# Moving the middle half groups of the down projection among the products of an FFN pass on one Trainium2 core

## The chip, the core and the metric

The kernel runs on one core of a Trainium2 chip. The metric is the device time of one execution in microseconds (us); lower is better. TensorE multiplies matrices into PSUM, VectorE and ScalarE read PSUM and do the elementwise work, GpSimd has a small part, and SyncE (SP) issues the DMAs that bring weights from HBM.

## The reference

A two-layer trunk over 528 tokens (16 meta tokens and 512 inputs) of width 1024. Layer 0 has a sparse attention, layer 1 a differential attention, and each layer ends with the same gated FFN with a causal convolution of width 3. The change concerns that FFN alone:

```python
def conv_ffn(h, w_up, conv_w, conv_b, w_down):      # w_up: 1024 x 5632, w_down: 2816 x 1024
    u = h @ w_up
    up = jnp.pad(u, ((0, 0), (CONV_W - 1, 0), (0, 0)))
    c = conv_b + sum(up[:, j:j + Tp] * conv_w[j] for j in range(CONV_W))
    gate, val = jnp.split(c, 2, axis=-1)
    return (jax.nn.silu(gate) * val) @ w_down
```

## The kernel before

Activations lie with features on the 128 partitions and tokens along the free dimension. Float32 products are made of three matmuls each, from a high and a low part of either operand: a cast on ScalarE gives the high part (`hi`, L168), a subtraction on VectorE the low one (`lo`, L176).

The FFN has 22 blocks of 128 features f. Blocks 0 and 1 are computed plainly; f = 2 to 21 go through `up_pair(f)`, one pass for each. A pass computes the gate block and the value block of f together, for two halves of the tokens, by seven products in place of eight (the scheme of Strassen and Winograd). A product (`product`, its matmuls are L1240) is 4 steps in the contraction of three matmuls: 12 matmuls of 264 columns in layer 0, of 258 in layer 1. The names used here, in the order before the change:

- P1: G times the first half of the inputs, into g0. ScalarE then copies g0 to v0 (L1270), so that later products can add to it.
- P5: the sum weights S12 times input sums, into g1. ScalarE copies g1 to the tile p5 (L1274).
- P6: the other half of S12, added onto v0. VectorE then sets g1 = v0 + p5 (L1279).
- P2: the other half of G, added onto g0.
- P3: S34, onto v0; VectorE then sets v1 = v0 + p5 (L1296).
- P4: S34, onto g1. Now g is finished and goes through the convolution (`convolve`: ScalarE L1328, VectorE L1331).
- P7, the last product: half of the value weights (A22), onto v0. Then v is convolved.

g0 and g1 are two halves of one PSUM tile g, in two of its banks; v0 and v1 likewise of v.

While the passes run, the down projection of finished blocks is done beside them. `down(p, m)` multiplies four finished blocks by one of the 8 output blocks m, in two half groups of two blocks, and then adds the result to h on VectorE (L1385). It is a generator: the first `next` issues the first half group, the second `next` the other half, the third the addition. A half group (its matmuls are L1374) is 12 matmuls in layer 0, where the 528 tokens are taken in two pieces of 272 and 256 columns, and 6 of 512 columns in layer 1. Passes f = 5 to 20 have a "middle" pair of half groups (`at_mid`, generator `a`), passes f = 4 to 19 a "late" pair (`at_late`, generator `b`), one half behind P4 and one behind P7.

Inside the passes the order on TensorE, VectorE and ScalarE is the order of the code (`manual_schedule`, L1453); the other engines are ordered by the scheduler of the framework. The weights are handled by two objects of class `Weights`: `wt` for G, S12 and S34, `ws` for the half groups and A22, each with three buffers in turn for the raw weights, the high parts and the low parts. `early` issues the cast on ScalarE, `late` the low part on VectorE, `sum` two of the additions that make S12 and S34 (L137 and L138, L141 and L142), `take` hands weights to a product, `done` gives their buffers back, and a load is issued on SP (L115) when its raw buffer is free.

Of the kernel before, what the change touches and what calls it, by code (L numbers as in the profile page):

```python
# [229 lines left out]
def mm_cost(n):  # L230
    return n / 2400 + 0.003


class Trunk:
# [929 lines left out]
    def ffn(self, l):  # L1164
# [4 lines left out]
        wt, ws, x = self.wt, self.wsm, self.next_x  # L1169
# [5 lines left out]
        with self.pool("fp") as fp:  # L1175
# [61 lines left out]
            def product(out, w, wk, xs, xk, c0, first=True):  # L1237
                for k in range(4):
                    for p, (wi, xi) in enumerate(((0, 0), (0, 1), (1, 0))):
                        nc.tensor.matmul(out, w[wi][:, wk + k, :], xs[xi][:, xk + k, c0:c0 + N],  # L1240
                                         start=(first and k == 0 and p == 0), stop=(k == 3 and p == 2), skip_group_check=not first)
                    self.pe(3 * mm_cost(N))
                    self.poll()

            def up_pair(f):

                x0, x1 = x[0][2:], x[1][2:]
                off = 512 - mid
                more = f + 1 < NF
                n3, ns = wt.taken, ws.taken
                a, b = ((z.get(f) and down(*z[f])) or iter(()) for z in (at_mid, at_late))
                g = ps.tile([128, 1024], F32, tag="sp", name="g")
                g0, g1 = g[:, off + st0:512], g[:, 512:512 + N]
                for i in range(ns, ns + (f in at_mid) + (f in at_late) + 1):  # L1260
                    ws.early(i)
                before = rest.pop(f - 1, iter(()))
                next(before, None)
                while ws.half:
                    ws.late()
                G, S12 = wt.take(), wt.take()
                product(g0, G, 0, x0, 0, st0)
                v = ps.tile([128, 1024], F32, tag="sp", name="v")
                v0, v1 = v[:, off + st0:512], v[:, 512:512 + N]
                nc.scalar.copy(v0, g0)  # L1270
                next(before, None)
                product(g1, S12, 0, TT[0], 0, 0)
                p5 = fp.tile([128, 264], F32, tag="p", name="p5", bufs=2)[:, :N]
                nc.scalar.copy(p5, g1)  # L1274
                if more:
                    wt.sum()
                next(a, None)
                product(v0, S12, 4, TT[1], 0, 0, False)
                nc.vector.tensor_tensor(g1, v0, p5, op=OP.add)  # L1279
                if more:  # L1280
                    wt.sum()
                product(g0, G, 4, x0, 4, st0, False)
                wt.done()
                wt.done()
                wt.early(n3 + 3)
                wt.late()
                wt.early(n3 + 4)
                next(a, None)
                next(a, None)
                if f in at_mid:  # L1290
                    ws.done()
                if f + 1 in at_mid:
                    ws.early(ws.taken + (f in at_late) + 1)
                S34 = wt.take()
                product(v0, S34, 0, TT[2], 0, 0, False)
                nc.vector.tensor_tensor(v1, v0, p5, op=OP.add)  # L1296
                wt.late()
                ws.late()
                product(g1, S34, 4, x1, 4, mid - 264, False)
                wt.done()  # L1300
                convolve(g, f, 0, off)
                wt.early(n3 + 5)
                wt.late()
                next(b, None)
                nc.scalar.activation(conv[0][:, :n], conv[0][:, :n], AF.Silu)
                A22 = ws.take()
                product(v0, A22, 0, TT[3], 0, 0, False)
                convolve(v, f, 1, off)
                next(b, None)
                if f in at_late:  # L1310
                    ws.done()
                ws.done()
                rest[f] = finish_pair(f, conv[0], conv[1], b)
# [3 lines left out]
            def finish_pair(f, c, t, b):  # L1317
                nc.vector.tensor_tensor(c[:, :n], c[:, :n], t[:, :n], op=OP.mult)
                next(b, None)
                yield  # L1320
                split_acts(f, c)
                yield

            def convolve(u, f, e, off=240):
                j = f + NF * e
                w0, w1, w2, b = (par[:, cb + 44 * q + j:cb + 44 * q + j + 1] for q in range(4))
                t = conv[e] = fp.tile([128, T], F32, tag=f"c{e}", name=f"c{e}", bufs=2)
                nc.scalar.activation(t[:, :n], u[:, off + t0:off + T], AF.Identity, bias=b, scale=w2)  # L1328
                for d, w in ((1, w1), (2, w0)):
                    z = d if l == 0 else 0  # L1330
                    nc.vector.scalar_tensor_tensor(t[:, z:n], u[:, off + t0 + z - d:off + T - d], w, t[:, z:n],  # L1331
                                                   op0=OP.mult, op1=OP.add)
# [66 lines left out]
            def down(p, m):  # L1399
                f0, f1 = self.PARTS[p]  # L1400
                t, w = new(), ws.take()
                for k in range(f1 - f0):
                    if k == (f1 - f0) // 2:
                        yield
                    block(t, w, f0 + k, k, cols, k == 0, k == f1 - f0 - 1)
                yield
                add(t, m, cols, False)
                yield
# [34 lines left out]
            at_late, at_mid = self.down_slots()  # L1443
# [9 lines left out]
            with self.tc.manual_schedule(engines=ENGINES):  # L1453
                for f in range(self.PLAIN, NF):
                    up_pair(f)
                for _ in rest.pop(NF - 1):
                    pass
# [479 lines left out]
```

## Time and profile before

| | |
|---|---|
| median of 3 runs | 1424.27 us (1422.84 to 1425.43) |
| the profiled execution | 1424.05 us |
| its span | 1422.2 us |
| TensorE matmul busy | 1303.1 us (92%) |
| VectorE busy | 1076.8 us (76%) |
| ScalarE busy | 689.8 us (49%) |
| granted TensorE clock, mean | 0.977 |

The span is the time from the first to the last instruction that the profiler saw; the execution's own time has some 1.9 us around it. Passes f = 5 to 20 lie at 350 to 632 us in layer 0 and at 1097 to 1371 us in layer 1. In a timeline row, the text in brackets at the end is the time that the engine stood idle ahead of the instruction, with the instruction that it waited for. Matmuls are pipelined: each row is longer than the distance to the next start, and its end is modelled.

### The profile page before, as it was taken

How to read it: one execution, taken by the hardware profiler on the slowest of the kernel's cores; microseconds unless marked ns; L12 is line 12 of the kernel's file. 1: busy time of each engine (PE TensorE's matmuls, PEld its weight loads, DVE VectorE, ACT ScalarE, POOL GpSimd, SP SyncE). 2: the span in 40 equal slices, each digit the busy share in tenths (PEclk: the TensorE clock that was granted, in tenths of full speed). 3: DMA queues.
4: the chain of work that ended last, by engine and by line, in shares of the span. 5: the costliest groups of instructions: out<-in, count | busy, mean ns of one | idle time of the engine just before them, and what ended most of it. 6: DMA issues, size and time to landing. Idle time of an engine off the chain costs nothing.

```text
span 1422.2 us, 24955 instructions
## 1 busy us (share of the span) xinstructions
PE 1303.1 (92%) x9688; PEld 1238.2 (87%) x9688; DVE 1076.8 (76%) x2126; ACT 689.8 (49%) x1330; POOL 286.8 (20%) x334
## 2 busy tenths in 40 slices
PE   5999899988999999989799999999888999999988
PEld 4999788887999999989799999989787888888886
DVE  6499977788888888876657777665888888888873
ACT  4453555564444444444445555554564444444441
POOL 3404442400000000003444552445400000000000
PEclk9999999999999999999999999989999999999999
DMA  7312221221223322213222322112222332223212
GB/s 227 116 60 85 74 84 57 82 82 60 91 90 89 94 91 91 75 55 103 90 66 80 91 66 69 48 34 86 79 82 61 102 90 92 89 90 95 83 56 93
DMA packets 49302, 118.98 MB, mean 84 GB/s; under 512 B 6192, under 2 KB 15712, under 8 KB 49184
## 3 DMA queue, kind: packets, MB, share of 16 engines
q1 hardware_dynamic: 48432, 114.57, 26.2%
q0 software_dynamic: 752, 2.82, 0.6%
q8 instruction: 76, 1.25, 0.4%
q14 instruction: 42, 0.34, 0.1%
HBM read 112.46 MB, written 4.91 MB: 83 GB/s over the span
## 4 chain that ended last, share of the span: by engine, by line
PE 77%; DVE 13%; ACT 5%; issue 3%; POOL 1%; DMA 1%; SPq 0%; ACTq 0%; DVEq 0%; POOLq 0%
PE lin L306 20%; PE g L1240 17%; PE dn L1374 17%; PE v L1240 12%; DVE c L1331 2%; PE pv L1742 1%; PE stq L681 1%; DVE g L1279 1%; DVE lo L176 1%; PE pv L1119 1%; ACT v L1270 1%; PE linh L306 1%; DVE acc L560 1%; ACT hi L168 1%; DVE xl L630 1%
## 5 line engine op out<-in xcount | busy, mean ns | idle before, releaser
L306 PE MATMUL lin<-xh,hi 128*128 128x256 f32 (+3 forms) x928 | 271.9, 298 | 13.0 <-DVE ht L547 6.4
L306 PE MATMUL lin<-xl,hi 128*128 128x256 f32 (+3 forms) x928 | 272.0, 294 | 3.3 <-DVE xl L630 1.7
L306 PE MATMUL lin<-xh,lo 128*128 128x256 f32 (+3 forms) x928 | 271.6, 294 | 0.0
L168 ACT CAST hi<-raw 128x1024 fp32r<-128x1024 f32 (+3 forms) x225 | 181.5, 822 | 176.6 <-PE v L1240 81.9
L176 DVE TENSOR_TENSOR lo<-raw,hi 128x512 fp32r<-128x512 f32 (+3 forms) x196 | 177.8, 922 | 21.0 <-ACT hi L168 18.1
L306 PEld LDWEIGHTS lin<-xh,hi 128*128 128x128 f32 (+1 forms) x928 | 179.1, 195 | 16.7 <-ACT xh L656 8.5
L306 PEld LDWEIGHTS lin<-xl,hi 128*128 128x128 f32 (+1 forms) x928 | 180.9, 195 | 5.0 <-DVE xl L630 3.1
L306 PEld LDWEIGHTS lin<-xh,lo 128*128 128x128 f32 (+1 forms) x928 | 180.9, 195 | 0.0
L1240 PE MATMUL g<-xh,hi 128*128 128x264 f32 (+1 forms) x480 | 140.7, 293 | 30.8 <-DVE g L1279 24.1
L1374 PE MATMUL dn<-al,hi 128*128 128x256 f32 (+2 forms) x528 | 142.7, 321 | 0.0
L1374 PE MATMUL dn<-ah,lo 128*128 128x256 f32 (+2 forms) x528 | 142.4, 321 | 0.0
L1374 PE MATMUL dn<-ah,hi 128*128 128x256 f32 (+2 forms) x528 | 142.3, 321 | 0.0
L1240 PE MATMUL v<-Th,lo 128*128 128x264 f32 (+1 forms) x480 | 136.3, 284 | 0.0
L1240 PE MATMUL v<-Tl,hi 128*128 128x264 f32 (+1 forms) x480 | 136.2, 284 | 0.0
L1240 PE MATMUL v<-Th,hi 128*128 128x264 f32 (+1 forms) x480 | 135.9, 283 | 0.0
L1240 PE MATMUL g<-xl,hi 128*128 128x264 f32 (+1 forms) x480 | 135.8, 283 | 0.0
L1240 PE MATMUL g<-xh,lo 128*128 128x264 f32 (+1 forms) x480 | 135.8, 283 | 0.0
L1240 PEld LDWEIGHTS g<-xh,hi 128*128 128x128 f32 x480 | 90.3, 188 | 40.9 <-DVE g L1279 32.5
L168 ACT CAST hi<-S 128x1024 fp32r<-128x1024 f32 x80 | 83.5, 1043 | 49.5 <-PE g L1240 48.1
L1385 DVE TENSOR_TENSOR ht<-dn,ht 128x256 f32<-128x256 f32 (+2 forms) x120 | 58.2, 514 | 54.2 <-PE dn L1374 54.2
L176 DVE TENSOR_TENSOR lo<-S,hi 128x1024 fp32r<-128x1024 f32 x80 | 97.3, 1217 | 0.0
L1374 PEld LDWEIGHTS dn<-ah,lo 128*128 128x128 f32 x528 | 89.1, 188 | 7.6
(299 smaller groups left out, 3257.5 us busy)
## 6 DMA issues: line engine op xcount, KB each, us to landing
raw<-w_up SPq DMA_DIRECT2D x88, 512.0 KB, 3.6
raw<-w_down SPq DMA_DIRECT2D x64, 256.0 KB, 2.7
raw<-w_in SPq DMA_DIRECT2D x16, 512.0 KB, 3.6
raw<-w_kv SPq DMA_DIRECT2D x16, 512.0 KB, 3.6
raw<-w_down SPq DMA_DIRECT2D x16, 384.0 KB, 3.2
nb<-nbias SPq DMA_DIRECT2D x16, 264.0 KB, 2.8
raw<-w_o_a SPq DMA_DIRECT2D x8, 512.0 KB, 3.7
raw<-w_q SPq DMA_DIRECT2D x8, 512.0 KB, 3.5
```

Of the source, the lines that this page charges most:

```text
L168: nc.scalar.copy(hi[:, :n, :m], src)
L176: eng.tensor_tensor(lt[:, :n, :m], src, hi[:, :n, :m].bitcast(F32), op=OP.subtract)
L306: i = self.nc.tensor.matmul(o, w[wi][:, kw + k, :m], x[s][xi][:, kx + k, c0:HN[s]], start=(first and p == 0), stop=(last and p == 2))
L560: eng.tensor_tensor(acc, acc, sq[:, :n], op=OP.add)
L630: i = eng.tensor_tensor(xl[:, m, o:o + n], xfs[m][:, :n], xh[:, m, o:o + n].bitcast(F32), op=OP.subtract)
L681: self.nc.tensor.matmul(st[:, c:c + 2], sq[:, c0:c0 + 128], rhs, start=True, stop=True)
L1119: nc.tensor.matmul(pv[:, :4 * nq], v[:, c, :], pp[:, :, :nq], start=(ci == 0 and p == 0), stop=(ci == nch - 1 and p == 2))
L1240: nc.tensor.matmul(out, w[wi][:, wk + k, :], xs[xi][:, xk + k, c0:c0 + N], start=(first and k == 0 and p == 0), stop=(k == 3 and p == 2), ...
L1270: nc.scalar.copy(v0, g0)
L1331: nc.vector.scalar_tensor_tensor(t[:, z:n], u[:, off + t0 + z - d:off + T - d], w, t[:, z:n], op0=OP.mult, op1=OP.add)
L1374: nc.tensor.matmul(part(t, c0, c1, o), w[wi][:, k, :], acts[f][ai][:, c0:c1], start=(first and p == 0), stop=(last and p == 2))
L1385: nc.vector.tensor_tensor(hv, part(t, c0, c1, o), hv, op=OP.add)
```

## The change

In each pass the first middle half group moves from behind P5 to the place in front of P5, and the second half group, with the addition to h that follows it, moves from behind P2 to the place in front of P2. The order of groups becomes P1, half group, P5, P6, half group, P2. The calls on `ws` that stood behind the second half group (`done`, the `early` for the next pass's middle weights) move with it, and the `ws.late()` that belongs to this `early` moves there from its place behind the addition of v1.

```diff
                 nc.scalar.copy(v0, g0)
                 next(before, None)
+                next(a, None)
                 product(g1, S12, 0, TT[0], 0, 0)
                 p5 = fp.tile([128, 264], F32, tag="p", name="p5", bufs=2)[:, :N]
                 nc.scalar.copy(p5, g1)
                 if more:
                     wt.sum()
-                next(a, None)
                 product(v0, S12, 4, TT[1], 0, 0, False)
                 nc.vector.tensor_tensor(g1, v0, p5, op=OP.add)
                 if more:
                     wt.sum()
+                next(a, None)
+                next(a, None)
+                if f in at_mid:
+                    ws.done()
+                if f + 1 in at_mid:
+                    ws.early(ws.taken + (f in at_late) + 1)
+                    ws.late()
                 product(g0, G, 4, x0, 4, st0, False)
                 wt.done()
                 wt.done()
                 wt.early(n3 + 3)
                 wt.late()
                 wt.early(n3 + 4)
-                next(a, None)
-                next(a, None)
-                if f in at_mid:
-                    ws.done()
-                if f + 1 in at_mid:
-                    ws.early(ws.taken + (f in at_late) + 1)
                 S34 = wt.take()
                 product(v0, S34, 0, TT[2], 0, 0, False)
                 nc.vector.tensor_tensor(v1, v0, p5, op=OP.add)
                 wt.late()
-                ws.late()
                 product(g1, S34, 4, x1, 4, mid - 264, False)
```

## Rows read from the trace of the kernel before

**Rows 1.** The page, part 1: span, busy time of each engine.

```profile
span 1422.2 us, 24955 instructions
PE 1303.1 (92%) x9688; PEld 1238.2 (87%) x9688; DVE 1076.8 (76%) x2126; ACT 689.8 (49%) x1330; POOL 286.8 (20%) x334
```

**Rows 2.** Waits: engine and line, releaser, us in total, times, longest.

```profile
PE g L1240 <- ACT v L1270: 27.4, 40, 1.7
...
PE g L1240 <- DVE g L1279: 24.1, 40, 0.8
```

**Rows 3.** Timeline, TensorE, pass of layer 0: start, duration, instruction, idle before.

```profile
491.72 0.28 PE L1240 MATMUL g<-xh,hi 128*128 128x264 f32 x1
...
493.04 0.28 PE L1240 MATMUL g<-xh,lo 128*128 128x264 f32 x1
493.82 0.39 PE L1240 MATMUL g<-Th,hi 128*128 128x264 f32 x1 [0.50 <-ACT v L1270]
494.05 0.29 PE L1240 MATMUL g<-Tl,hi 128*128 128x264 f32 x1
...
495.40 0.41 PE L1374 MATMUL dn<-ah,hi 128*128 128x256 f32 x2
...
496.86 0.28 PE L1240 MATMUL v<-Th,hi 128*128 128x264 f32 x1
...
498.18 0.28 PE L1240 MATMUL v<-Th,lo 128*128 128x264 f32 x1
499.06 0.39 PE L1240 MATMUL g<-xh,hi 128*128 128x264 f32 x1 [0.60 <-DVE g L1279]
...
509.40 0.28 PE L1240 MATMUL g<-xh,hi 128*128 128x264 f32 x1
```

**Rows 4.** Timeline, TensorE, pass of layer 1.

```profile
1253.48 0.28 PE L1240 MATMUL g<-xh,lo 128*128 128x258 f32 x1
1254.25 0.39 PE L1240 MATMUL g<-Th,hi 128*128 128x258 f32 x1 [0.49 <-ACT v L1270]
...
1255.81 0.40 PE L1374 MATMUL dn<-ah,hi 128*128 128x512 f32 x1
...
1257.19 0.28 PE L1240 MATMUL v<-Th,hi 128*128 128x258 f32 x1
...
1258.52 0.28 PE L1240 MATMUL v<-Th,lo 128*128 128x258 f32 x1
1259.39 0.38 PE L1240 MATMUL g<-xh,hi 128*128 128x258 f32 x1 [0.60 <-DVE g L1279]
```

**Rows 5.** Timeline, TensorE, pass f = 3 of layer 0, without half groups.

```profile
324.54 0.29 PE L1240 MATMUL g<-Th,lo 128*128 128x264 f32 x1
324.66 0.28 PE L1240 MATMUL v<-Th,hi 128*128 128x264 f32 x1
...
326.87 0.39 PE L1240 MATMUL g<-xh,hi 128*128 128x264 f32 x1 [0.60 <-DVE g L1279]
```

**Rows 6.** Timeline, VectorE, the pass of rows 3.

```profile
496.85 0.69 DVE L138 TENSOR_TENSOR S<-S,raw 128x512 f32<-128x512 f32 x1
498.57 0.44 DVE L1279 TENSOR_TENSOR g<-v,p 128x264 f32<-128x264 f32 x1 [1.03 <-PE v L1240]
...
500.12 1.22 DVE L176 TENSOR_TENSOR lo<-raw,hi 128x1024 fp32r<-128x1024 f32 x1
502.17 0.77 DVE L1385 TENSOR_TENSOR ht<-dn,ht 128x256 f32<-128x256 f32 x2 [0.83 <-PE dn L1374]
503.76 0.44 DVE L1296 TENSOR_TENSOR v<-v,p 128x264 f32<-128x264 f32 x1 [0.82 <-PE v L1240]
...
505.24 0.69 DVE L176 TENSOR_TENSOR lo<-raw,hi 128x512 fp32r<-128x512 f32 x1
```

**Rows 7.** Busy time by stretch: engines in order, granted clock, DMA share, GB/s.

```profile
350.12:631.99 281.87, 262.86 (x2091) 255.92 (x2089) 228.19 (x350) 127.65 (x189) 0.00 (x0) 1.00 0.28 85
...
646.00:681.00 35.00, 34.92 (x287) 34.69 (x285) 24.12 (x34) 14.89 (x28) 14.23 (x10) 1.00 0.32 98
```

## What was predicted, before the changed kernel had run

> **What bounds the kernel now.** I read the page first: TensorE is busy for 1303.1 us of 1422.2, VectorE for 1076.8, ScalarE for 689.8 [rows 1]. TensorE is the bound, so what counts is where it stands still. The table of waits names two stops inside the passes of `up_pair`, 40 times each: the first matmul of a product waits for the ScalarE copy of L1270 (v0 from g0), and another for the VectorE add of L1279 (g1 = v0 + p5) [rows 2]. By the order of the code the first is P5, the second P2. Third, the TensorE timeline of one pass of each layer, to price the stops [rows 3, 4].
>
> There one must not take the idle time in brackets (0.50 and 0.60 us). A matmul row is 0.28 us long, but in a running stream they start every 0.12 us, so much of a stop lies under the modelled end of the last row. I go by starts. In layer 0, last matmul of P1 at 493.04, first of P5 at 493.82: 0.78 instead of 0.12, lost 0.66. The next one starts at 494.05, 0.23 later instead of 0.12: 0.11 more for starting again. At P2: 498.18 to 499.06 is 0.88, lost 0.76, and 0.11 again (the same pattern). Together 0.66 + 0.11 + 0.76 + 0.11 = 1.64 us per pass [rows 3]. Cross-check: the pass takes 509.40 - 491.72 = 17.68 us and holds eleven groups (seven products, or parts of one, and four half groups); a half group takes 496.86 - 495.40 = 1.46, and eleven times that is 16.06, so 1.62 are lost [rows 3]. In layer 1: 1254.25 - 1253.48 = 0.77 and 1259.39 - 1258.52 = 0.87, so 0.65 + 0.11 + 0.75 + 0.11 = 1.62 [rows 4].
>
> **What the change does, part by part.** No instruction is added or removed. In the 16 passes f = 5 to 20 of each layer (32 in all) that have a middle half group pair, the first half group goes from behind P5 to in front of it, the second from behind P2 to in front of it, and with the second go its addition to h (L1385, VectorE), the release of its weights, and the cast (ScalarE) and low part (VectorE) of the next pass's half group weights. In the other passes only the cast and low part can move.
>
> *First half group in front of P5.* The copy of g0 needs P1 alone, so it now runs beside the half group. P5 could start 0.78 us after the last start of P1; with the half group between it comes up 0.12 + 1.46 = 1.58 us after it. The copy may be 0.80 us late before P5 notices; in layer 1, where a half group takes 1257.19 - 1255.81 = 1.38, it is 1.50 - 0.77 = 0.73 [rows 3, 4]. Gain: 0.77 in layer 0, 0.76 in layer 1. If that cover were gone, this is what comes back.
>
> *P6 straight behind P5, P3 straight behind P2.* These neighbours are new in the 32 passes, but pass f = 3, which has no half groups, has them already: last of P5 at 324.54, first of P6 at 324.66, 0.12 us, no stop [rows 5]. P6 sums onto v0, which was there before P5 ran. Cost 0. The copy of g1 into p5 now has only P6 to hide behind. That too is so in f = 3, where P6 to P2 shows the same stop of 0.60 us. Cost 0.
>
> *Second half group in front of P2.* P2 comes up 1.58 us after the last start of P6 and could start after 0.88: the VectorE add has 0.70 us in hand, 0.63 in layer 1 [rows 3, 4]. Is VectorE there in time? It ended the sums ahead of the add at 496.85 + 0.69 = 497.54 and stood idle 1.03 us for P6 [rows 6]. P6 now ends 0.77 us sooner, so 0.26 of that is left, and the add still starts with P6's end. VectorE may come 0.26 + 0.70 = 0.96 us later than it did before P2 waits at all. Gain 0.87 in layer 0, 0.86 in layer 1.
>
> *The moved addition and low part.* VectorE works in order, so from now on the addition to h (0.77) waits for the second half group with the low part of the half group weights (0.69), of the next G (1.22) and the add of v1 behind it. Between the sums of L141 and L142 and v1's add there were 503.76 - 500.12 = 3.64 us, with 1.22 + 0.77 = 1.99 of work and 1.65 idle; the pass loses 0.87 us here, so 2.77 us are left for 2.68 of work [rows 6]. This is the tightest place. But a late v1 add delays nobody until the last product, two groups on (P4 and a late half group), 2.9 us; and the low part of 0.69 leaves the stretch in front of the convolution. [...] I take 0, upper bound 0.25 us per pass (about what VectorE had left at P2), 8 us in all. Below 0 I see nothing: TensorE waits for none of it now.
>
> *The moved cast on ScalarE* takes the place of the weights that the second half group has read, so it waits for that group as before, and now stands ahead of the casts of G and S12 instead of behind. ScalarE is busy 127.65 of 281.87 us in these passes [rows 7]; G's low part is needed only at the next pass. Cost 0. *The DMAs:* the load that this releases goes to SP's queue ahead of the next load of w_up, where it stood behind; with three raw buffers in turn and two loads of w_down a pass, what is cast here was asked for a pass earlier. Cost 0; were a load late, the cast and all behind it on ScalarE would wait, and that is priced as lateness of VectorE below. GpSimd has nothing in this stretch [rows 7].
>
> **The sum.** 16 × 1.64 + 16 × 1.62 = 52.2 us. The profiled execution took 1424.05 us, so 1371.9; the median of the runs shown, 1424.27, is 0.2 us above it: 1372.
>
> **The rivals.**
>
> *Less comes back* (0.12). If the idle column were the truth, the gain would be 16 × 1.10 + 16 × 1.09 = 35 us, 1389. Against it stand the starts and the length of the pass; for it, that the restart of 0.11 us might stay where the engine changes between products and half groups (the changes that the trace shows cost 0.12, like any other start). A VectorE lateness just over the 0.96 us falls in here too: 1380 to 1389.
>
> *Only one stop goes* (0.03). If P5 waits for something else of the same moment, only the stop at P2 goes: 16 × 0.87 + 16 × 0.86 = 27.7, 1396. Against it: the waits name one releaser in all 40 cases. [...]
>
> *Nothing changes* (0.02). The order in the code would be moved and the stops with it, for example by a wait of P6 directly behind P5: 1424. The start of P6 in f = 3 speaks against it [rows 5].
>
> *Slower* (0.03). VectorE becomes the bound: its queue, held at the head by the addition to h, arrives at the add of L1279 later from pass to pass. Place: P2. It decides from 0.96 us on, and eats up the whole gain at 0.96 + 1.64 = 2.6 us per pass. At 3.5 us the kernel would be 32 × 0.9 = 29 us slower, 1453. Against it: VectorE is busy 228.19 of 281.87 us in these passes, 14.3 us of a pass that would last 16.06 [rows 7]. For it: that is 89%, with waits in between.
>
> That TensorE's clock would fall in a closer stream I leave without a chance of its own: where the stream has no stops already (34.92 of 35 us busy), the granted clock is 1.00, as in the passes [rows 7].
>
> **How the numbers follow.** The forecast has 0.80 and its own range is 1367 to 1380 (the sum less the 8 us above; and below it 5 us, an estimate of a tenth of the gain, for work elsewhere that falls into another order). With most of the first rival the range is 1366 to 1389, which leaves out about 0.12. Faster by over 0.2% (some 3 us, about what a measurement of this kernel can tell from no change) are forecast, first and second rival: 0.95; same 0.02; slower 0.03.
>
> **What would show it.** In the profile after: P5 and P2 starting 0.12 us behind a half group; the two waits [rows 2] down from 40 cases to the 8 passes without a middle pair; a pass of layer 0 of 16.06 us; VectorE idle in front of L1279 near 0.3 us and next to none in front of L1296. I am wrong if P2 still waits for L1279 (VectorE late), if P6 or P3 starts with a stop, or if the passes shorten and a later stage lengthens.

## The result, and the profile after

The changed kernel takes 1371.49 us, median of 4 (1368.6 to 1372.15), against 1423.69 (1422.84 to 1425.43) of the kernel before on the same chip: the ratio is 0.9628, with a 95% interval of 0.9611 to 0.9645. The prediction said 1372. Medians here leave out one execution, the fourth of the kernel with the second half group alone, which took 4337.78 us where its other three took 1390 to 1394.

The profiled execution has a span of 1369.8 us, 52.4 less than before. Cut into stages at the first matmul of P1 of pass f = 5 and of pass f = 21 in each layer, it shows where the time came from (us, from the TensorE timelines):

| stage | before | after | difference |
|---|---|---|---|
| up to P1 of f = 5, layer 0 | 350.12 | 350.57 | +0.45 |
| passes 5 to 20, layer 0 | 281.87 | 255.39 | -26.48 |
| f = 21, end of layer 0, mixer of layer 1, up to P1 of f = 5, layer 1 | 464.87 | 462.65 | -2.22 |
| passes 5 to 20, layer 1 | 274.55 | 248.60 | -25.95 |
| f = 21 and the end | 50.79 | 52.59 | +1.80 |

All of it lies in the 32 passes: 26.48 + 25.95 = 52.43 us, where 52.2 had been worked out. The rest adds up to nothing.

First the busy time by stretch, for the same two stretches of passes (columns as in [rows 7]):

```profile
350.57:605.96 255.39, 254.27 (x2091) 254.09 (x2089) 226.55 (x350) 126.04 (x189) 0.00 (x0) 1.00 0.31 94
1068.61:1317.21 248.60, 247.51 (x1717) 231.17 (x1716) 222.26 (x318) 124.88 (x189) 0.00 (x0) 1.00 0.31 96
```

TensorE is now busy 254.27 of 255.39 us in layer 0, and the 1.12 us that are missing are a single stop at the end, ahead of P1 of f = 21. VectorE does the same work (226.55 us, 228.19 before) in less time: 89% busy instead of 81%.

The timeline of TensorE in one pass of layer 0, which answers [rows 3]; a row is start, duration, instruction, and the idle time before it if there was any:

```profile
482.00 0.29 PE L1240 MATMUL g<-Th,hi 128*128 128x264 f32 x1
482.12 0.29 PE L1240 MATMUL g<-Tl,hi 128*128 128x264 f32 x1
...
483.46 0.28 PE L1240 MATMUL v<-Th,hi 128*128 128x264 f32 x1
...
486.14 0.40 PE L1374 MATMUL dn<-ah,lo 128*128 128x256 f32 x2
486.37 0.28 PE L1240 MATMUL g<-xh,hi 128*128 128x264 f32 x1
486.50 0.28 PE L1240 MATMUL g<-xl,hi 128*128 128x264 f32 x1
...
498.05 0.29 PE L1240 MATMUL g<-Th,hi 128*128 128x264 f32 x1
```

P5 begins at 482.00 and in the next pass at 498.05: the pass takes 16.05 us, before it was 17.68. P6 follows straight on P5 (483.46), and P2 on the half group: 486.37, 0.23 us after a row that stands for two matmuls. No row has a bracket, and the first matmul of P5 and of P2 is 0.28 or 0.29 us long and followed 0.12 or 0.13 us later, where it was 0.39 and 0.23: the restart is gone with the stop.

The table of waits (engine, line, releaser; us in total, times, longest), against [rows 2]:

```profile
PE g L1240 <- ACT v L1270: 11.6, 8, 1.9
...
PE g L1240 <- DVE g L1279: 4.7, 8, 0.6
```

Forty cases have become eight: f = 2, 3, 4 and 21 of both layers, which have no middle pair.

The timeline of VectorE in the same pass, against [rows 6]:

```profile
484.21 0.69 DVE L138 TENSOR_TENSOR S<-S,raw 128x512 f32<-128x512 f32 x1
485.18 0.44 DVE L1279 TENSOR_TENSOR g<-v,p 128x264 f32<-128x264 f32 x1 [0.28 <-PE v L1240]
485.53 0.68 DVE L141 TENSOR_TENSOR S<-raw,S 128x512 f32<-128x512 f32 x1
486.13 0.68 DVE L142 TENSOR_TENSOR S<-raw 128x512 f32<-128x512 f32 x1
486.73 0.76 DVE L1385 TENSOR_TENSOR ht<-dn,ht 128x256 f32<-128x256 f32 x2
487.42 1.82 DVE L176 TENSOR_TENSOR lo<-raw,hi 128x512 fp32r<-128x512 f32 x2
489.50 0.44 DVE L1297 TENSOR_TENSOR v<-v,p 128x264 f32<-128x264 f32 x1 [0.27 <-PE v L1240]
```

In front of L1279 VectorE is idle for 0.28 us (1.03 before); in front of L1385, the moved addition to h, it does not wait at all (0.83 before); in front of the add of v1 (now L1297) for 0.27 us. It is still the one that waits for TensorE, not the other way round.

### The profile page after: what moved, and what is told of

The parts are those of the page before. It is cut to its first block, busy times and chain, and to the rows that moved or that the text cites. A ratio compares the mean times of both kernels' runs of the same rounds, so it can differ in the third digit from the quotient of the medians.

```text
span 1369.8 us, 24924 instructions
## 1 busy us (share of the span) xinstructions
PE 1288.9 (94%) x9688; PEld 1237.9 (90%) x9688; DVE 1071.4 (78%) x2126; ACT 685.4 (50%) x1330; POOL 286.5 (21%) x334
## 4 chain that ended last, share of the span: by engine, by line
PE 82%; DVE 10%; ACT 4%; issue 2%; POOL 1%; DMA 1%; SPq 0%; ACTq 0%; DVEq 0%; POOLq 0%
PE lin L306 22%; PE dn L1374 18%; PE g L1240 17%; PE v L1240 12%; DVE c L1331 2%; PE stq L681 1%; PE pv L1742 1%; PE linh L306 1%; PE pv L1119 1%; DVE xl L630 1%; ACT hi L168 1%; PE sa L1024 1%; PE pt L1756 1%; PE stk L671 1%; PE sb L1668 1%
## 5 line engine op out<-in xcount | busy, mean ns | idle before, releaser
L168 ACT CAST hi<-raw 128x512 fp32r<-128x512 f32 (+3 forms) x225 | 178.6, 822 | 161.6 <-PE dn L1374 88.8
L176 DVE TENSOR_TENSOR lo<-raw,hi 128x1024 fp32r<-128x1024 f32 (+3 forms) x196 | 175.1, 921 | 21.8 <-ACT hi L168 18.9
L1240 PE MATMUL g<-xh,hi 128*128 128x264 f32 (+1 forms) x480 | 137.2, 286 | 11.3 <-DVE c L1331 6.6
L1374 PEld LDWEIGHTS dn<-ah,hi 128*128 128x128 f32 x528 | 88.8, 188 | 5.7 <-ACT hi L168 1.1
L1374 PEld LDWEIGHTS dn<-al,hi 128*128 128x128 f32 x528 | 89.2, 189 | 4.8
```

Of the source, the lines that this page charges most:

```text
L168: nc.scalar.copy(hi[:, :n, :m], src)
L176: eng.tensor_tensor(lt[:, :n, :m], src, hi[:, :n, :m].bitcast(F32), op=OP.subtract)
L1374: nc.tensor.matmul(part(t, c0, c1, o), w[wi][:, k, :], acts[f][ai][:, c0:c1], start=(first and p == 0), stop=(last and p == 2))
```

## The experiments

The theory: each stop is a wait for which nothing was put beside it, a half group covers the one that it stands in front of, and VectorE keeps up. The rivals: the two moves work only together; the stop at P5 is for something else than the shared tile; VectorE is as good as the bound; the gain goes with the length of the cover. Whole times scatter by up to 10 us between executions (the kernel before took 1418.03 to 1428.20 us on one chip), and in the profiles most of that lies outside the passes: the stretch from f = 21 of layer 0 to f = 5 of layer 1 took between 456 and 465 us in kernels that edit nothing in it. So I read the passes 5 to 20, whose granted clock is 1.00 in every profile. In one profiled execution of each kernel they add up to (us, layer 0 + layer 1, against the kernel before and against the changed one):

| kernel | passes 5 to 20 | to before | to after | whole, median | ratio to before (95%) |
|---|---|---|---|---|---|
| before | 281.87 + 274.55 = 556.42 | | | 1423.69 | |
| after | 255.39 + 248.60 = 503.99 | -52.43 | | 1371.49 | 0.9628 (0.9611 to 0.9645) |
| first half group alone | 269.05 + 262.62 = 531.67 | -24.75 | | 1392.75 | 0.9800 (0.9765 to 0.9836) |
| second half group alone | 267.65 + 260.97 = 528.62 | -27.80 | | 1392.43 | 0.9786 (0.9754 to 0.9817) |
| before, P5 in an own bank | 269.46 + 262.41 = 531.87 | -24.55 | | 1386.10 | 0.9740 (0.9713 to 0.9767) |
| after, P5 in an own bank | 255.38 + 248.61 = 503.99 | | 0.00 | 1356.58 | 0.9535 (0.9501 to 0.9570) |
| after, 1 VectorE addition more | 255.38 + 248.61 = 503.99 | | 0.00 | 1366.43 | 0.9603 (0.9573 to 0.9634) |
| after, 2 VectorE additions more | 260.88 + 254.89 = 515.77 | | +11.78 | 1381.72 | 0.9706 (0.9681 to 0.9730) |
| after, middle pair in quarters | 257.71 + 252.48 = 510.19 | | +6.20 | 1373.32 | 0.9653 (0.9621 to 0.9684) |
| after, once more | 255.39 + 248.60 = 503.99 | | 0.00 | 1368.96 | 0.9608 (0.9587 to 0.9629) |
| after, outer passes with own bank | 255.39 + 248.61 = 504.00 | | +0.01 | 1362.07 | 0.9563 (0.9542 to 0.9583) |
| the same, P2 ahead of P6 there | 255.38 + 248.61 = 503.99 | | 0.00 | 1353.64 | 0.9501 (0.9481 to 0.9522) |

### One half group at a time

To the order before, the first half group alone:

```diff
                 next(before, None)
+                next(a, None)
                 product(g1, S12, 0, TT[0], 0, 0)
...
-                next(a, None)
                 product(v0, S12, 4, TT[1], 0, 0, False)
```

> Only the first half group is moved, in front of P5; the second stays behind P2. Theory (each stop is a wait without cover, and each half group covers the one behind it): the stop at P5 goes in 32 passes, the stop at P2 stays at 0.60 us by the idle column. Gain 16 x 0.77 + 16 x 0.76 = 24.5 us, about 1399. Rival (the two moves only work together, for instance because VectorE meets P6 too late once P6 comes sooner): the stop at P2 grows by what the one at P5 loses, about 1424.

To the order after, the first half group back behind P5, so that only the second is moved:

```diff
                 next(before, None)
-                next(a, None)
                 product(g1, S12, 0, TT[0], 0, 0)
...
+                next(a, None)
                 product(v0, S12, 4, TT[1], 0, 0, False)
```

> Only the second half group, with its addition to h and the cast and low part of the next weights, is moved in front of P2; the first stays behind P5. Theory: the stop at P2 goes in 32 passes, the stop at P5 stays at 0.50 us by the idle column. Gain 16 x 0.87 + 16 x 0.86 = 27.7 us, about 1396; with the gain of the first half alone it adds up to the 52.2 us of the whole. Rival (the two moves only work together): clearly less than 27.7.

In the passes the first won 24.75 us (24.5 expected), the second 27.80 (27.7 expected); together 52.55, against 52.43 for both at once. The moves are independent, and the rival that they work only together falls. In the first of the two kernels the stop at P2 is the old one, not a longer one. Its timeline:

```profile
490.29 0.28 PE L1240 MATMUL v<-Th,lo 128*128 128x264 f32 x1
491.17 0.39 PE L1240 MATMUL g<-xh,hi 128*128 128x264 f32 x1 [0.60 <-DVE g L1279]
```

It is again 0.88 us between the starts and 0.60 in the bracket, although P6 came 0.77 us sooner: VectorE was in time. By whole time the two kernels win 31.3 and 31.7 us against the 1424.08 us of the kernel before beside them; what goes beyond 24.75 and 27.80 lies outside the passes, where nothing was edited, within the scatter named above.

### The stop at P5 without any half group

The order before, with P5 in a PSUM bank of its own:

```diff
-                product(g1, S12, 0, TT[0], 0, 0)
+                q5 = ps.tile([128, 512], F32, tag="one", name="q5")[:, :N]
+                product(q5, S12, 0, TT[0], 0, 0)
...
-                nc.scalar.copy(p5, g1)
+                nc.scalar.copy(p5, q5)
```

> The order of before, but P5 goes into a PSUM bank of its own instead of the second half of the tile g. Theory (P5 waits for the copy of g0 only because both lie in one tile, not for data): the stop at P5 goes without any half group being moved, 24.5 us in the 32 passes; in passes f = 3, 4 and 21 P6 then waits for the copy, some 0.5 us instead of 2.0, so another 6 to 9 us. Together about 1391; the stop at P2 stays. Rival (P5 waits for something else of that moment): 1424, the stop only has another place.

The same edit in the kernel after:

> The changed kernel with P5 in a PSUM bank of its own. Theory: in the 32 passes nothing is left to win at P5; in the passes without a middle pair some 1.4 us each for f = 3, 4 and 21 of both layers, less for f = 2: 6 to 10 us under the changed kernel, 1362 to 1366. Rival (the bank that P5 takes from the half groups makes them wait): the changed kernel's 1371.5 or more, with stops at the first matmul of a half group.

In these two kernels no matmul writes g1 ahead of P4, and they leave out of g what VectorE put into g1; only their time is read (the number and kind of instructions is that of the full computation). The first won 24.55 us in the passes, as much as moving the first half group (24.75). P5 now starts straight behind P1:

```profile
484.40 0.29 PE L1240 MATMUL g<-xh,lo 128*128 128x264 f32 x1
484.52 0.29 PE L1240 MATMUL q<-Th,hi 128*128 128x264 f32 x1
```

P5 starts 0.12 us after the last matmul of P1 (484.52 after 484.40), and its matmuls go on at 0.12 or 0.13 us each up to the half group at 486.00. In the kernel before, the copy of g0 ran 0.37 us after the start of the last matmul of P1 and took 0.36 (493.41 against 493.04); at the same distance it would lie here at 484.77 to 485.13, beside P5, which is an estimate. So P5 never needed the copy of g0: the stop came with the shared tile, which is all that the edit takes away. Whether two results in one tile could have done without the wait, no run shows. In the kernel after, the own bank changes nothing in the passes 5 to 20 (503.99 both), as expected: the same stop cannot be won twice. It does shorten the outer passes, f = 2 to 4: 47.79 instead of 50.03 us in layer 0, 45.97 instead of 50.46 in layer 1. But passes 3 and 4 win only 0.40 to 0.41 us each, where 1.4 each was expected. The stops of pass f = 3 in the kernel after, and then with the own bank:

```profile
323.53 0.39 PE L1240 MATMUL g<-Th,hi 128*128 128x264 f32 x1 [1.71 <-ACT v L1270]
327.31 0.39 PE L1240 MATMUL g<-xh,hi 128*128 128x264 f32 x1 [0.60 <-DVE g L1279]
```

```profile
319.88 0.39 PE L1240 MATMUL v<-Th,hi 128*128 128x264 f32 x1 [0.22 <-ACT v L1270]
323.24 0.39 PE L1240 MATMUL g<-xh,hi 128*128 128x264 f32 x1 [1.63 <-DVE g L1280]
```

Most of the stop at P5 comes back at P2, because VectorE has no idle time left in front of its add there: with the own bank L1280 starts at 322.75, 0.61 us behind L138, with no idle marked. The rest of the gain lies in f = 2, and in layer 0 it goes with the clock. Passes 2 to 4 of layer 0 in the kernel after, in the kernel with one VectorE addition more (shown below; the same code in these passes), and in the kernel after with the own bank (columns as in [rows 7]):

```profile
300.54:350.57 50.03, 40.23 (x300) 38.30 (x299) 40.28 (x61) 26.17 (x42) 0.00 (x0) 0.97 0.19 58
298.39:346.92 48.53, 38.74 (x301) 36.82 (x299) 40.28 (x61) 26.18 (x42) 0.00 (x0) 1.00 0.19 60
298.31:346.10 47.79, 38.88 (x301) 36.84 (x299) 40.18 (x61) 25.66 (x42) 0.00 (x0) 1.00 0.19 61
```

With the clock at 1.00 in both, the own bank is worth 0.74 us; the other 1.50 is the clock. The whole time of the kernel after with the own bank, 15 us under the changed kernel, goes beyond the 6 to 10 expected. The outer passes f = 2 to 4 and the end (49.72 instead of 52.59) make 9.6 of it, with a granted clock of 0.97, 0.93 and 0.96 in the changed kernel and of 1.00, 1.00 and 0.99 here; the rest lies in stages where at most f = 21 of layer 0 is edited.

### How late VectorE may be

The kernel after, with one or two (`range(2)`) additions on a tile that nobody else uses, in VectorE's queue ahead of L1279:

```diff
+                if f in at_mid:
+                    for _ in range(1):
+                        nc.vector.tensor_tensor(junk, junk, junk, op=OP.add)
                 product(v0, S12, 4, TT[1], 0, 0, False)
...
+            junk = fp.tile([128, 512], F32, name="junk")
+            nc.vector.memset(junk, 0.0)
```

> The changed kernel with one addition of 128x512 on VectorE (about 0.69 us) put in its queue ahead of the add of L1279 in passes 5 to 20, on a tile that nobody else uses. Theory (VectorE may come 0.28 + 0.70 = 0.98 us later in layer 0, about 0.9 in layer 1, before P2 waits): no change, 1371.5 within 2 us, and no idle left in front of L1279. Rival (VectorE is as good as the bound): 32 x 0.7 = 22 us more, 1394.

> The same with two such additions (about 1.4 us a pass). Theory: the add of L1279 ends later than P2 comes up by 0.46 us in layer 0 and 0.54 in layer 1, and a stop costs 0.11 more for starting again: 16 x 0.57 + 16 x 0.65 = 19.5 us, 1391, with a wait of P2 for L1279 in every such pass. Rival 1 (VectorE works this off elsewhere in the pass): 1371.5. Rival 2 (every us on VectorE counts): 32 x 1.4 = 45 us, 1416.

One addition costs nothing in the passes (503.99), two cost 11.78 us: 5.49 in layer 0 and 6.29 in layer 1. A pass of f = 5 takes 16.41 instead of 16.05 us in layer 0 and 16.06 instead of 15.63 in layer 1; f = 20, which has no late pair, loses nothing. The limit lies between one addition and two, as the theory wants; VectorE is not the bound, and not every us on it counts. The size was expected higher, 19.5. The timeline of VectorE with two additions shows why:

```profile
485.62 0.69 DVE L137 TENSOR_TENSOR S<-raw 128x512 f32<-128x512 f32 x1
486.35 0.69 DVE L138 TENSOR_TENSOR S<-S,raw 128x512 f32<-128x512 f32 x1
486.96 1.41 DVE L1280 TENSOR_TENSOR junk<-junk 128x512 f32<-128x512 f32 x2
488.29 0.43 DVE L1282 TENSOR_TENSOR g<-v,p 128x264 f32<-128x264 f32 x1
```

From 486.35 to 486.96 is 0.61: an addition of 0.69 us holds the next one up for 0.6 only, as matmul rows also overlap (0.28 us long, 0.12 apart). Where the next one reads its result, as L138 does with that of L137 and the second addition with that of the first, it is 0.72 to 0.73. So the two additions put L1279 back by 1.33 us (486.96 to 488.29; in this kernel the add is L1282), not by 1.4. What VectorE has in hand is more by starts, too: in the kernel after, L1279 could have followed L138 at 484.21 + 0.61 = 484.82 and started at 485.18, so 0.36 + 0.70 = 1.06 in layer 0, and 0.37 + 0.63 = 1.00 in layer 1. That leaves 0.27 and 0.33 us of lateness, with 0.11 for starting again 0.38 and 0.44 a pass; the 15 passes f = 5 to 19 would then lose 12.3 us, and 11.78 were measured. This sum was made after the run. On TensorE, in the same pass, P2 starts late behind the half group:

```profile
488.28 0.40 PE L1379 MATMUL dn<-ah,lo 128*128 128x256 f32 x2
488.77 0.39 PE L1240 MATMUL g<-xh,hi 128*128 128x264 f32 x1
489.00 0.28 PE L1240 MATMUL g<-xl,hi 128*128 128x264 f32 x1
```

0.49 us after a row of two matmuls, where the rows before it follow each other at 0.24 or 0.25, and the next 0.23 later: the stop of L1279, small, without any idle in a bracket. The modelled ends hide it wholly.

### How long a cover must be

The kernel after, with the middle pair in four quarters:

```diff
-            def down(p, m):
+            def down(p, m, cuts=(2,)):
...
-                    if k == (f1 - f0) // 2:
+                    if k in cuts:
...
+                next(a, None)
                 product(v0, S12, 4, TT[1], 0, 0, False)
...
+                next(a, None)
+                product(g0, G, 4, x0, 4, st0, False)
                 next(a, None)
                 next(a, None)
...
-                product(g0, G, 4, x0, 4, st0, False)
```

The middle pairs are cut at (1, 2, 3); the calls on `ws` stand behind the addition.

> The middle pair of half groups in four quarters of 6 matmuls (3 of 512 columns in layer 1): one in front of P5, one behind it, one in front of P2, one behind it, with the addition to h and the cast and low part of the next weights behind that. Theory (a cover need only be as long as the wait): a quarter covers 0.12 + 0.73 = 0.85 us in layer 0 and 0.81 in layer 1. P5 needs 0.78 and 0.77: no stop. P2 needs 0.88 and 0.87: 0.03 to 0.06 short, and 0.11 for starting again. In all 0 to 5 us over the changed kernel, 1371 to 1377. Rival (the gain goes with the length of the cover): half of the 52 us is lost, 1397.

It lost 6.20 us of the 52.43, a little over the 0 to 5 expected and far from half. In layer 1, where the quarter is 0.69 us, both stops come back a little:

```profile
1196.73 0.40 PE L1376 MATMUL dn<-ah,lo 128*128 128x512 f32 x1
1196.97 0.35 PE L1240 MATMUL g<-Th,hi 128*128 128x258 f32 x1
1197.15 0.28 PE L1240 MATMUL g<-Tl,hi 128*128 128x258 f32 x1
...
1201.09 0.40 PE L1376 MATMUL dn<-ah,lo 128*128 128x512 f32 x1
1201.38 0.39 PE L1240 MATMUL g<-xh,hi 128*128 128x258 f32 x1
1201.61 0.28 PE L1240 MATMUL g<-xl,hi 128*128 128x258 f32 x1
```

P5 starts 0.24 behind the last matmul of the quarter, on time, but its second matmul comes 0.18 later instead of 0.12: with 0.04 us in hand the restart already shows in part. P2 is late by 0.06 and pays 0.11 more. In layer 0, where P5 has 0.07 in hand, its second matmul still comes 0.16 later. What was in hand and what was still paid make 0.10 and 0.11 us, so by an estimate from these two a cover must be as long as the wait and about 0.1 us more; the whole half group (1.46 and 1.38 us) has 0.6 to 0.8 us to spare, nearly half of it is not needed.

### A kernel that beats both

What is left in these FFN passes are the stops of f = 2, 3, 4 and 21. The first of two kernels gives P5 its own bank there, with one matmul more that writes g1 ahead of VectorE's add, so that P4 adds to it:

```diff
+                q5 = g1
+                if f not in at_mid:
+                    q5 = ps.tile([128, 512], F32, tag="one", name="q5")[:, :N]
-                product(g1, S12, 0, TT[0], 0, 0)
+                product(q5, S12, 0, TT[0], 0, 0)
...
-                nc.scalar.copy(p5, g1)
+                nc.scalar.copy(p5, q5)
...
+                if f not in at_mid:
+                    nc.tensor.matmul(g1, S12[0][:, 3, :], TT[0][0][:, 3, :N], start=True, stop=True)
                 product(v0, S12, 4, TT[1], 0, 0, False)
```

The second has P2 ahead of that matmul and of P6 in the same four passes. Both ran beside the changed kernel:

> The changed kernel once more, unaltered, beside the next two on the same chip: 1371.5 within 3 us, passes 5 to 20 together 504.0 us as in its first profile.

> The changed kernel; in the passes without a middle pair (f = 2, 3, 4 and 21) P5 goes into a PSUM bank of its own, and one matmul more opens g1 for P4. Theory (P5 waits there only for the shared tile): passes 5 to 20 stay as they are; the outer passes lose 2.2, 3.4, 1.1 and 1.1 us as in the kernel that had the bank in all passes, and get 8 x 0.12 = 1.0 us for the added matmul: 6.8 us under the changed kernel, about 1364.7. Rival (the added matmul on g1 waits for the copy in P5's place): no change.

> As the one before, and in the same four passes P2 goes ahead of P6. Theory: P2 now fills the time in which VectorE is not yet free for the add of L1279; the stop of 1.6 us at P2 becomes one of 0.9 us at P3 and P6 no longer stands in front of it. About 1.2 us less in each of f = 3, 4 and 21 of both layers: 7 us, 1357.5. Rival (P3 waits for the add as long as P2 did): the same as the kernel before.

The changed kernel took 1368.96 us here (1366.34 to 1370.72), 2.5 under its first median, with the same 503.99 us in the passes. The first of the two took 1362.07, 6.9 us under it; the second 1353.64 (1350.67 to 1356.23), 8.4 under the first and 15.3 under the changed kernel; its ratio to the kernel before is 0.9501 (0.9481 to 0.9522). Passes 2 to 4 took 49.93 and 49.38 us in the changed kernel, 47.77 and 46.91 in the first, 44.63 and 43.80 in the second.

That the first came out at the 6.8 us expected is partly luck, for that sum was taken from passes that had differed in their clock. Passes 3 and 4 win 0.40 to 0.44 us each; f = 2 wins 1.34 and 1.59, while the mean granted clock of passes 2 to 4 goes from 0.97 to 1.00 in both layers. P2 ahead of P6, with the clock at 1.00 in both kernels, wins 0.9 us in each of f = 3 and 4 (1.2 expected) and 1.3 in f = 2, which no sum had. The stops of pass f = 3 with the own bank in all passes, and then with P2 first:

```profile
316.48 0.36 PE L1240 MATMUL g<-xh,hi 128*128 128x264 f32 x1 [1.12 <-DVE c L1332]
319.88 0.39 PE L1240 MATMUL v<-Th,hi 128*128 128x264 f32 x1 [0.22 <-ACT v L1270]
323.24 0.39 PE L1240 MATMUL g<-xh,hi 128*128 128x264 f32 x1 [1.63 <-DVE g L1280]
```

```profile
313.68 0.36 PE L1240 MATMUL g<-xh,hi 128*128 128x264 f32 x1 [1.05 <-DVE c L1338]
317.08 0.39 PE L1240 MATMUL g<-xh,hi 128*128 128x264 f32 x1 [0.23 <-ACT v L1270]
321.00 0.39 PE L1240 MATMUL v<-Th,hi 128*128 128x264 f32 x1 [0.60 <-DVE g L1285]
```

The stop for VectorE's add went from 1.63 us, at P2, to 0.60 at P3, because P2 and P6 now both run before the add is needed. The 1.05 ahead of P1, until VectorE has convolved g of the pass before, stays.

## Why the prediction was right

*The sum.* The passes gave 26.48 and 25.95 us; 26.2 and 25.9 had been worked out, 1.64 and 1.62 a pass. The step that carried it was to go by starts and not by the idle column. By the idle column the gain would have been 35 us; the restart of 0.11 and the part of the stop under the modelled end of a row were real and came back in full. That rival ("less comes back") has fallen. Of the 26.48, some 0.25 is a single pass of the kernel before that took 17.97 us; a usual pass went from 17.68 or 17.73 to 16.05 or 16.08.

*First half group.* 24.75 us alone, 24.5 predicted. *Second half group.* 27.80 alone, 27.7 predicted. *New neighbours* P5 to P6 and P2 to P3: no stop, as the pass f = 3 had shown [rows 5].

*VectorE.* 0.26 us left in front of L1279 were predicted, 0.28 measured; the limit of 0.96 us lies between the two runs with added work, 0.60 and 1.33 us. By starts it is 1.06, and the loss of the second fits that. The tightest place was estimated too tight: in front of the add of v1 0.09 us were to be left, and there were 0.27. The three pieces of work there were counted by their durations (2.68 us), but their starts follow each other from 486.73 to 489.24 (the modelled end of the last), 2.5 us. It is the same slip that made the expectation for two more additions too high: as the matmul rows of 0.28 us follow each other at 0.12, so the additions of 0.69 us do at 0.61, where the next does not read their result. Here it cost nothing, since the place was priced at 0 either way. That VectorE takes its work in the order of the code shows in the kernel before: it stood idle for 0.82 us until the add of v1 at 503.76, though the cast for the low part behind it (504.11) had ended on ScalarE at 501.76.

*ScalarE, the loads, the clock.* Nothing in the passes waits for the moved cast (among the waits between 351 and 604 us and between 1069 and 1316 us none names a cast as the releaser); the granted clock stayed at 1.00 in the closer stream of passes 5 to 20.

*The rival of one stop only* rested on the question whether P5 waits for the tile. It does, and the run with the own bank shows it: 24.55 us without moving anything.

*The rest of the program.* An estimate of 5 us had been left for work elsewhere; -2.22, +0.45 and +1.80 are what it was, and they cancel. That the whole time of 1371.49 us meets the forecast to within 1 us is partly luck: the same kernel, run again, took 1368.96.

## What to carry to other kernels

Price a stop of TensorE by the distance between starts, minus the usual distance, plus the same for the instruction after it; the idle time in a row's bracket shows only two thirds of it (1.10 of 1.64 us here), and a short stop not at all (0.25 us at P2 with two additions more). Independent work of the same engine that already lies nearby is worth most directly in front of the instruction that waits (24.75 and 27.80 us here), and it need be only as long as the wait and 0.1 us more (the estimate from the quarters). Before moving work, ask whether the wait is for data or only for a tile that two results share; where it is the tile, another buffer wins the same time (24.55 us here) and leaves the cover free for a stop that is real. Look first at what the next stop waits for: in passes 5 to 20 of the kernel before the own bank won 0.77 us a pass, in f = 3 and 4, where VectorE had no idle time in front of its add, 0.4.

## What the hardware showed that was not expected

In the changed kernel's first profile the last pass of layer 1 (f = 21) ran 15 matmuls at a start distance of 0.21 to 0.22 us instead of 0.12. The stretches around it (engines in order, then granted clock, DMA share, GB/s):

```profile
1318.00:1321.00 3.00, 1.12 (x9) 0.92 (x8) 2.69 (x5) 1.54 (x4) 0.00 (x0) 0.97 0.02 5
1321.00:1324.00 3.00, 3.00 (x15) 3.00 (x16) 0.99 (x2) 0.61 (x2) 0.00 (x0) 0.50 0.46 132
1324.00:1328.00 4.00, 3.40 (x27) 3.20 (x27) 1.39 (x2) 1.31 (x3) 0.00 (x0) 0.97 0.00 2
```

For three microseconds the granted clock was 0.50. Ahead of it TensorE had stood still for 1.09 us and, after the 12 matmuls of P1, for 1.88 us. It made up most of the +1.80 us of that stage: in the repeat the end took 51.09 us instead of 52.59, at the same code. There the two stops were the same, 1.09 and 1.88 us, and the clock stayed at 1.00 behind them, as it did in the kernel before with stops of 1.09 and 1.62. So the length of the stops alone does not decide it; what does stays open.

The outer passes show the same cost more often. Over passes 2 to 4 of a layer the mean granted clock was 0.93 or 0.97 in 15 of the 16 stretches of kernels in which P5 shares the tile there (two layers, eight profiles), and 1.00 in all 8 stretches of the kernels with the own bank. So stops that are as short as these came with a cost beyond their own length (in f = 2 of layer 0 of the changed kernel, stops of 1.78 and 0.61 us, and behind them 12 matmuls that start 0.21 to 0.23 us apart): 1.50 us in layer 0, twice the 0.74 that the own bank took out directly. That the own bank is what keeps the clock up is a reading of these counts, not of an experiment made for it. In the passes 5 to 20, before and after, with and without their stops, the granted clock was 1.00 in every profile.
